# A two-level Strassen matmul: the product S3 x T3 by seven quarter products too, four weight quarters fetched again from DRAM, half of C scaled at the end

## The chip, the core and the metric

The kernel runs on one core of a Trainium2 chip. The metric is the device time of one execution, in microseconds. Before the change it is 1456.46 us, the median of three runs (1455.99 to 1456.82).

## The reference

```python
def setup_inputs():
    B, S, D = 8, 2048, 2048
    return {
        "x": np.random.randn(B, S, D).astype(np.float32),
        "w": np.random.randn(D, D).astype(np.float32),
    }

def reference(x, w):
    cs = np.cumsum(x, axis=1)
    diff = cs - np.concatenate([np.zeros(...), cs[:, :-1, :]], axis=1)
    return np.matmul(diff, w).astype(np.float32)
```

A running sum and the difference of neighbours cancel, so what is computed is x w: 16384 x 2048 by 2048 x 2048, in float32.

## The kernel before

**Tiles.** x is cut into 128 row tiles of 128 rows. The weights stay in SBUF as float16 sums (`W`). Four row tiles make a group, named g, h, k, l. g and h are the upper half of the outer Strassen scheme's A, k and l the lower one; the columns of x give the other division. After 12 tiles that are worked by other functions, 29 groups (class `Group`) remain.

**A group.** The outer scheme has seven products, P1 to P7. Each is 256 x 1024 by 1024 x 1024 and is worked either whole (`Group.whole`, 32 matmuls of 128x512) or by an inner Strassen scheme: seven quarter products p1 to p7 of four matmuls each (`quarter`, L570), with four small sums s1 to s4 of quarter rows (`small_sums`, L1001). P1 to P5 are worked by seven, P6 (S2 x T2) and P7 (S3 x T3) whole.

**Weight quarters.** An inner scheme needs sums of weight quarters. Most stand in `W` or `inner`. Six of them are made anew for each group by one VectorE operation of 128x2048 into the buffer `flow` (`fill_by`, L934; steps `P1.fp4`, `P2.fp4`, `P3.fp2`, `P4.fp4`, `P5.fp4`, `P5.fp5`) and read by the quarter product of that name.

**Results.** A 128x512 piece of C starts as a scaled copy out of a PSUM bank (`keep`, ScalarE, L580), takes further products by scaled adds (`add`, VectorE, L583: c = bank * u + c), and is stored by `put` (L594). `merge` (L1027) adds a copy of one bank to another bank, and `copy` (L1020) takes such a copy, where one product serves several sums (`by_seven`, P1 and P5).

**Rows of x.** `load` fetches a tile in two halves of 512 KB, the first to one of three places of the buffer `F`, the second to one of two others (L101). `weigh` takes the sum of magnitudes (ScalarE), `scale_of` a maximum and its reciprocal (VectorE), `unit_of` the factor for C (GpSimd), `narrow` writes float16 in place (ScalarE), `turn` transposes by DMA.

**What sets the order.** `ORDER` (L1195) is a list of step names, written out, that is gone through once per group; `+1` or `+2` says how many groups ahead a step belongs. `after` chains each engine's instructions in just this order, so each engine has a fixed queue. All loads, stores and transposes are issued by SyncE (SP), in one queue too. PSUM banks are taken from and given back to `open_banks`, pieces of C to `free`, small sums to `scratch`. The last group ends by `END_ORDER`.

## Time and profile before

| | |
|---|---|
| median of three runs | 1456.46 us |
| span of the profiled execution | 1455.0 us |
| instructions | 20120 |
| HBM read, written | 150.99 MB, 134.22 MB |
| bytes moved by DMA, mean rate | 351.59 MB, 242 GB/s |

The profile is one execution. Busy time of an engine is the union of its instructions' times; times of matmuls are pipelined and their ends modelled. An instruction's line (L584) can be that of a helper: all scaled adds into C have L584, all quarter products L573, the whole products L554, the small and large sums of x L544, the fills L937, the merges in PSUM L1030. "DMA share" is the mean busy share of the core's 16 DMA engines. Each idle time names what ended it.

### The profile page before, as it was taken

The page shows a single profiled execution, that of the slowest core. Times are in us where ns is not written, and L with a number is a line of the kernel's source. Part 1 is how long each engine was busy: PE and PEld are TensorE (multiplying, and loading weights), DVE is VectorE, ACT ScalarE, POOL GpSimd, SP SyncE. Part 2 cuts the span into 40 slices and gives each one's busy share as a digit, 9 for nine tenths or more (in the row PEclk, how much of TensorE's full clock was granted, in tenths as well). Part 3 has the DMA queues.
Part 4 walks back from the last instruction along what each step waited for, and adds up shares of the span by engine and source line. Part 5 has one row for each costly group of instructions (what it writes and reads, how often), then busy time and mean ns, then how long its engine had stood idle before and what let it go on. Part 6 is the DMA issues. An engine that isn't in the chain of part 4 may idle for free.

```text
span 1455.0 us, 20120 instructions
## 1 busy us (share of the span) xinstructions
PE 1441.1 (99%) x6673; PEld 652.6 (45%) x6679; DVE 1333.3 (92%) x2302; ACT 967.5 (66%) x1446; POOL 48.6 (3%) x136
## 2 busy tenths in 40 slices
PE   8999999999999999999999999999999999999998
PEld 3444444444444444444444444444444444444443
DVE  7998899999999999999999999999999999999998
ACT  5887656676666666667666667766666766666662
POOL 0111000000000000000000000000000000000000
PEclk9999999999999999999999999999999999999999
DMA  9999868898888998878998888998878898888983
GB/s 360 367 240 299 236 171 234 248 246 232 234 237 237 248 253 230 235 236 233 260 241 233 231 228 240 260 238 241 225 235 247 247 233 239 226 244 246 253 203 123
DMA packets 377752, 351.59 MB, mean 242 GB/s; under 512 B 274800, under 2 KB 274800, under 8 KB 377520
## 3 DMA queue, kind: packets, MB, share of 16 engines
q1 hardware_dynamic: 377088, 348.47, 84.9%
q0 software_dynamic: 560, 1.84, 0.3%
q8 instruction: 52, 0.85, 0.2%
q14 instruction: 52, 0.43, 0.1%
HBM read 150.99 MB, written 134.22 MB: 196 GB/s over the span
## 4 chain that ended last, share of the span: by engine, by line
PE 96%; DMA 2%; DVE 1%; issue 0%; ACT 0%; SPq 0%; DVEq 0%; ACTq 0%
PE b L573 61%; PE b L554 32%; PE b L275 2%; DMA W<-in_w_dram 1%; DMA W<-in_x_dram 1%; DVE c L584 1%; ACT wb L259 0%; PE b L400 0%; DVE x L544 0%; SPq L219 0%; DVE b L1030 0%; DVE flow L937 0%; DVE inner L544 0%; DVE W L541 0%; ACT c L581 0%
## 5 line engine op out<-in xcount | busy, mean ns | idle before, releaser
L584 DVE SCALAR_TENSOR_TENSOR c<-b,of,c 128x512 f32<-128x512 f32 x790 | 574.1, 747 | 74.3 <-PE b L573 64.3
L554 PE MATMUL b<-W,x 128*128 128x512 f16 x2144 | 506.6, 379 | 0.0
L581 ACT ACTIVATE c<-b,of 128x512 f32<-128x512 f32 x492 | 312.6, 680 | 230.9 <-PE b L573 113.3
L573 PE MATMUL b<-W,x 128*128 128x512 f16 x1892 | 452.4, 379 | 0.8 <-ACT b L1023 0.7
L158 ACT ACTIVATE F<-F,of 128x1024 f16<-128x1024 f32 x246 | 282.2, 1147 | 174.8 <-DVE of L141 172.6
L573 PEld LDWEIGHTS <-x 128*128 128x128 f16 x2488 | 243.4, 98 | 295.3 <-issue 2.7
L554 PEld LDWEIGHTS <-x 128*128 128x128 f16 x2144 | 209.8, 98 | 253.0 <-DVE x L544 0.2
L123 ACT ACTIVATE waste<-F 128x1024 uint8<-128x1024 f32 x246 | 259.3, 1054 | 4.6 <-DMA F<-in_x_dram 2.5
L573 PEld LDWEIGHTS <-inner 128*128 128x128 f16 x1648 | 161.2, 98 | 195.6 <-issue 1.3
L573 PE MATMUL b<-W,inner 128*128 128x512 f16 x944 | 242.2, 379 | 0.9 <-DVE b L1030 0.9
L544 DVE TENSOR_TENSOR x<-x,x 128x1024 f16<-128x1024 f16 (+1 forms) x388 | 226.6, 584 | 3.3
L573 PE MATMUL b<-flow,x 128*128 128x512 f16 x588 | 150.9, 379 | 0.0
L573 PE MATMUL b<-inner 128*128 128x512 f16 x472 | 121.1, 379 | 0.0
L937 DVE TENSOR_TENSOR flow<-W 128x2048 f16<-128x2048 f16 x87 | 105.8, 1216 | 0.0
L1030 DVE TENSOR_TENSOR b<-b,c 128x512 f32<-128x512 f32 x116 | 80.6, 695 | 13.9 <-PE b L573 13.9
L147 POOL TENSOR_SCALAR of<-of,uw 128x1 f32<-128x1 f32 x124 | 43.6, 370 | 1306.7 <-DVE of L139 704.1
L937 DVE TENSOR_TENSOR flow<-W,inner 128x2048 f16<-128x2048 f16 x58 | 70.8, 1220 | 0.0
L1023 ACT COPY c<-b 128x512 f32<-128x512 f32 x58 | 33.4, 576 | 51.3 <-PE b L573 51.3
L275 PE MATMUL b<-wb,xP 128*128 128x512 bf16 x234 | 57.0, 395 | 5.3 <-ACT wb L259 3.9
L544 DVE TENSOR_TENSOR inner<-x 128x512 f16<-128x512 f16 x117 | 49.4, 422 | 2.9 <-DMA x<-F 0.9
L1023 ACT COPY b<-b 128x512 f32<-128x512 f32 x87 | 51.2, 588 | 0.5 <-PE b L573 0.5
L544 DVE TENSOR_TENSOR inner<-x,inner 128x512 f16<-128x512 f16 x117 | 49.2, 421 | 2.0
(67 smaller groups left out, 530.0 us busy)
## 6 DMA issues: line engine op xcount, KB each, us to landing
F<-in_x_dram SPq DMA_DIRECT2D x246, 512.0 KB, 5.1
out_dram<-c SPq DMA_DIRECT2D x492, 256.0 KB, 3.0
W<-in_w_dram SPq DMA_DIRECT2D x32, 512.0 KB, 9.6
W<-in_x_dram SPq DMA_DIRECT2D x16, 256.0 KB, 7.2
x<-F SPq DMA_TRANSPOSE x246, 3.4
out_dram<-o POOLq DMA_DIRECT2D x5, 256.0 KB, 4.1
out_dram<-o SPq DMA_DIRECT2D x5, 256.0 KB, 3.5
xP<-in_x_dram SPq DMA_DIRECT2D x1, 1024.0 KB, 5.1
```

The costliest lines, as they stand in the source:

```text
L123: lambda: nc.scalar.activation(waste, where[t][i], ABS, scale=1.0 / ROW, accum_out=sums_of[t][:, i : i + 1],),
L147: after("pool", lambda: nc.gpsimd.tensor_scalar(u, m, uw, None, MUL))
L158: lambda: nc.scalar.activation(narrowed(t)[:, ds(i * NH, NH)], where[t][i], COPY, scale=s),
L275: lambda: nc.tensor.matmul(ps[r][n], xP[:, r, ko, :], wb[h, ko][:, ds(n * NB, NB)], start=(ko == 0), stop=(ko == KO - 1),),
L544: after("dve", lambda: nc.vector.tensor_tensor(dst.all, p.all, q.all, op))
L554: said = nc.tensor.matmul(to[n], a[k], b[k][:, n, :], start=(first and k == 0), stop=(k == KH - 1), skip_group_check=True,)
L573: said = nc.tensor.matmul(to, a[k], b[k], start=(first and k == 0), stop=(k == 3), skip_group_check=True)
L581: after("act", lambda: nc.scalar.activation(c, p, COPY, scale=u))
L584: after("dve", lambda: nc.vector.scalar_tensor_tensor(c, p, u, c, MUL, ADD))
L937: after("dve", lambda: nc.vector.tensor_tensor(in_twos(flow), x, y, op))
L1023: after("act", lambda: nc.scalar.copy(c, p))
L1030: after("dve", lambda: nc.vector.tensor_tensor(t, p, s, ADD))
```

## The change

P7 is worked by seven quarter products: `Inner(5, ...)` gives its weight quarters, `onto` is its plan. Unlike `by_seven`, `onto` adds into banks that already hold products: p1, p5, p6 and p7 are each copied out of a bank by ScalarE (`c1`, `c5`, `c6`, `c7`) and added to other banks by VectorE (six merges `a1` to `a7k`).

P7 has three passing weight quarters, which makes nine in a group. Four (P1.p4, P2.p4, P5.p5, P7.p4) use a second buffer, the third place of `F`. In the first group they are made by VectorE as before and stored in DRAM (`kept`); in later groups the same step is a DMA from there, issued by SP. From the twelfth x tile on, the first halves of x use two places of `F` instead of three.

For eight of the sixteen pieces of C (`LATE`), in all groups but the last, `keep` is a plain copy, `add` a plain PSUM plus SBUF add, and a new step `last` on ScalarE scales the piece in SBUF before its `put`. Maximum and reciprocal of a tile become two steps, `scale` and `recip`. `ORDER` is new as a whole. In the first group two sums that turn T3's quarters into what P7 needs stand ahead of P7.fp5.

```diff
--- before.py
+++ after.py
@@ -97,8 +97,10 @@
     queue_of_x = [PLAIN, PLAIN + 2, PLAIN + 3]
     for t in range(PLAIN + 4, END, 4):
         queue_of_x += [t, t + 2, t + 1, t + 3]
+    THREE = 11
     for i, t in enumerate(queue_of_x):
-        where[t] = [F[:, i % 3, :], F[:, 3 + i % 2, :]]
+        j = i % 3 if i < THREE else (i - THREE) % 2
+        where[t] = [F[:, j, :], F[:, 3 + i % 2, :]]
     unit = {}
     sums_of = {}
     scales = {}
@@ -129,7 +131,7 @@
                     ),
                 )
 
-    def scale_of(t):
+    def scale_of(t, apart=False):
         if t < END:
             m2 = sums_of.pop(t)
             m, s, u = (m2[:, i : i + 1] for i in (2, 3, 4))
@@ -138,12 +140,18 @@
                 "dve",
                 lambda: nc.vector.tensor_scalar(m, m2[:, :1], m2[:, 1:2], TINY, ADD, MAX),
             )
+            sizes[t] = m
+            if not apart:
+                recip_of(t)
+
+    def recip_of(t):
+        if t < END:
+            s, m = scales[t], sizes[t]
             after("dve", lambda: nc.vector.reciprocal(s, m))
-            sizes[t] = m
 
     def unit_of(t):
         if t < END:
-            u, m = unit[t], sizes.pop(t)
+            u, m = unit[t], sizes[t]
             after("pool", lambda: nc.gpsimd.tensor_scalar(u, m, uw, None, MUL))
 
     def narrowed(t):
@@ -517,7 +525,7 @@
                 p1=self.t11, p2=self.t21, p3=self.t22, p4=self.Q4,
                 p5=self.Q1, p6=self.Q2, p7=self.Q3,
             )
-            return {j: pieces_of(t) for j, t in places.items()}
+            return {j: pieces_of(t) for j, t in places.items() if t is not None}
 
     passed = [flow[:, k, :] for k in range(4)]
 
@@ -931,31 +939,60 @@
         put(C21h[0], h + 1, 0)
         turn(next_l, [1])
 
-    def fill_by(op, a, b):
-        def some():
-            x, y = (in_twos(t) for t in (a, b))
-            after("dve", lambda: nc.vector.tensor_tensor(in_twos(flow), x, y, op))
-
-        return some
-
+    kept = ctx.enter_context(tc.tile_pool(name="kept", bufs=1, space=bass.MemoryType.DRAM))
+    flows = [flow, F[:, 2, :].bitcast(f16).rearrange("p (k n) -> p k n", k=4)]
+
+    class Fill:
+        def __init__(self, op, a, b, again=False):
+            self.op, self.a, self.b = op, a, b
+            self.to = flows[again]
+            self.pieces = [self.to[:, k, :] for k in range(4)]
+            self.again = None
+            self.can = again
+
+        def __call__(self):
+            if self.again is not None:
+                after("sp", lambda: nc.sync.dma_start(self.to, self.again))
+                return
+            x, y = (in_twos(t) for t in (self.a, self.b))
+            after("dve", lambda: nc.vector.tensor_tensor(in_twos(self.to), x, y, self.op))
+            if self.can:
+                self.again = kept.tile([P, 4, NB], f16, name=f"kept{len(stored)}")
+                stored.append(self)
+                after("sp", lambda: nc.sync.dma_start(self.again, self.to))
+
+    stored = []
+
+    in_7 = Inner(5, None, quarter_of(5, 0, 1), None)
     sevens = {
-        "P1": (in_1, {"p4": fill_by(SUB, quarter_of(0, 1, 0), S1_all)}),
-        "P2": (in_2, {"p4": fill_by(SUB, quarter_of(4, 1, 0), inner[:, 8:12, :])}),
-        "P3": (in_3, {"p2": fill_by(ADD, spare_of(2, 0), inner[:, 16:20, :])}),
-        "P4": (in_4, {"p4": fill_by(SUB, quarter_of(7, 1, 0), spare_of(2, 4))}),
+        "P1": (in_1, {"p4": Fill(SUB, quarter_of(0, 1, 0), S1_all, again=True)}),
+        "P2": (in_2, {"p4": Fill(SUB, quarter_of(4, 1, 0), inner[:, 8:12, :], again=True)}),
+        "P3": (in_3, {"p2": Fill(ADD, spare_of(2, 0), inner[:, 16:20, :])}),
+        "P4": (in_4, {"p4": Fill(SUB, quarter_of(7, 1, 0), spare_of(2, 4))}),
         "P5": (
             in_5,
             {
-                "p4": fill_by(SUB, quarter_of(1, 1, 0), quarter_of(6, 1, 0)),
-                "p5": fill_by(SUB, quarter_of(1, 1, 1), quarter_of(6, 1, 0)),
+                "p4": Fill(SUB, quarter_of(1, 1, 0), quarter_of(6, 1, 0)),
+                "p5": Fill(SUB, quarter_of(1, 1, 1), quarter_of(6, 1, 0), again=True),
+            },
+        ),
+        "P7": (
+            in_7,
+            {
+                "p4": Fill(SUB, quarter_of(5, 1, 0), quarter_of(5, 0, 1), again=True),
+                "p5": Fill(SUB, quarter_of(5, 1, 1), quarter_of(5, 0, 1)),
+                "p7": Fill(SUB, quarter_of(5, 0, 1), quarter_of(5, 0, 0)),
             },
         ),
     }
     open_banks = []
     scratch = list(passing)
 
+    LATE = 'C12g0 C12g1 C12h1 C12h0 C11g1 C11h1 C21g1 C21h1'.split()
+
     class Group:
         def __init__(self, g):
+            self.late = LATE if g + 4 < END else ()
             self.tiles = dict(g=g, h=g + 2, k=g + 1, l=g + 3)
             self.at = {}
             self.do = {}
@@ -990,9 +1027,8 @@
 
             def some():
                 to, a = self.bank(b, fresh), self.sums[P][j]
-                quarter(
-                    to, self.real(a), passed if j in passes else inner.weights()[j], fresh
-                )
+                weights = passes[j].pieces if j in passes else inner.weights()[j]
+                quarter(to, self.real(a), weights, fresh)
                 if isinstance(a, str):
                     self.drop(a, scratch)
 
@@ -1046,25 +1082,64 @@
             self.quarter(P, "p3", g1, False)
             self.quarter(P, "p4", h0, False)
 
+        def onto(self, P, h0, h1, g0, g1):
+            q, e = f"{P}q", f"{P}e"
+
+            def snap(name, b, let=False):
+                def some():
+                    c, p = self.take(name, free), self.at[b]
+                    after("act", lambda: nc.scalar.copy(c, p))
+                    self.close(b, let)
+
+                return some
+
+            self.quarter(P, "p1", q, True)
+            self.step(f"{P}.c1", snap(f"{P}1", q))
+            self.merge(f"{P}.a1", g0, g0, f"{P}1", let=True)
+            self.quarter(P, "p2", g0, False)
+            self.quarter(P, "p5", e, True)
+            self.step(f"{P}.c5", snap(f"{P}5", e, True))
+            self.merge(f"{P}.a5g", g1, g1, f"{P}5")
+            self.merge(f"{P}.a5h", h1, h1, f"{P}5", let=True)
+            self.quarter(P, "p3", g1, False)
+            self.quarter(P, "p6", q, False)
+            self.step(f"{P}.c6", snap(f"{P}6", q))
+            self.merge(f"{P}.a6", g1, g1, f"{P}6", let=True)
+            self.quarter(P, "p7", q, False)
+            self.step(f"{P}.c7", snap(f"{P}7", q, True))
+            self.merge(f"{P}.a7h", h1, h1, f"{P}7")
+            self.merge(f"{P}.a7k", h0, h0, f"{P}7", let=True)
+            self.quarter(P, "p4", h0, False)
+
         def row(self, c):
             return self.tiles[c[3] if c[1] == "1" else {"g": "k", "h": "l"}[c[3]]]
 
         def keep(self, c, b, let=False):
             def some():
-                keep(self.take(c, free), self.at[b], unit[self.row(c)])
+                to, p, u = self.take(c, free), self.at[b], unit[self.row(c)]
+                if c in self.late:
+                    after("act", lambda: nc.scalar.copy(to, p))
+                else:
+                    keep(to, p, u)
                 self.close(b, let)
 
             self.step(f"keep.{c}", some)
 
         def add(self, c, b, tag, let=False):
             def some():
-                add(self.at[c], self.at[b], unit[self.row(c)])
+                to, p, u = self.at[c], self.at[b], unit[self.row(c)]
+                if c in self.late:
+                    after("dve", lambda: nc.vector.tensor_tensor(to, p, to, ADD))
+                else:
+                    add(to, p, u)
                 self.close(b, let)
 
             self.step(f"add.{c}.{tag}", some)
 
         def put(self, c):
             n = 2 * (c[2] == "2") + int(c[4])
+            if c in self.late:
+                self.step(f"last.{c}", lambda: keep(self.at[c], self.at[c], unit[self.row(c)]))
             self.step(f"put.{c}", lambda: put(self.at.pop(c), self.row(c), n))
 
         def plan(self):
@@ -1074,7 +1149,8 @@
                 self.step(f"load.{c}", lambda t=t: (load(t, 0), load(t, 1)))
                 self.step(f"weigh0.{c}", weigh, t, [0])
                 self.step(f"weigh1.{c}", weigh, t, [1])
-                self.step(f"scale.{c}", scale_of, t)
+                self.step(f"scale.{c}", scale_of, t, True)
+                self.step(f"recip.{c}", recip_of, t)
                 self.step(f"unit.{c}", unit_of, t)
                 self.step(f"narrow0.{c}", narrow, t, [0])
                 self.step(f"narrow1.{c}", narrow, t, [1])
@@ -1149,7 +1225,8 @@
             self.add("C12h1", q, "q")
             self.add("C12h0", q, "q", let=True)
 
-            self.whole("P7", T3, half["g"][0], half["h"][0], *x)
+            self.small_sums("P7", A("g", 0), A("h", 0), True)
+            self.onto("P7", *x)
             for n, c in zip(x, ("C22h0", "C22h1", "C22g0", "C22g1")):
                 self.add(c, n, "x")
 
@@ -1193,32 +1270,34 @@
                     self.step(f"{P}{c}.{j}", some, a, to, j)
 
     ORDER = """
...
+    weigh1.l+1 add.C11h1.e+1 scale.l+1 keep.C11g1+1 recip.l+1 P2.p6+1 P2.p2+1 P2.p3+1
+    narrow0.l+1 add.C11g1.q+1 S1.g+1 P2.p7+1 S2.g+1 add.C11g0.v+1 P5.p1+1 narrow1.l+1
+    add.C11g1.e+1 P6g.0+1 P6g.3+1 put.C12g1+0 add.C11h1.q+1 last.C21h1+0 P2.fp4+1
+    P3.fp2+1 P5.cg+1 last.C11h1+1 keep.C11h0+1 S4.g+1 P5.p2+1 P2.p4+1 turn0.l+1
+    turn1.l+1 S1.h+1 P5.s1+1 S2.h+1 last.C21g1+0 keep.C22g0+1 P6g.1+1 P6g.2+1 P3.p2+1
+    put.C11g0+1 P5.s2+1 last.C11g1+1 add.C11h0.q+1 load.g+2 P6h.0+1 P5.s3+1 P6h.3+1
+    P6h.1+1 P6h.2+1 S4.h+1 keep.C12g0+1 add.C12g0.z+1 P5.fp5+1 S3.g+1 weigh0.g+2 P4.s1+1
+    P7.p1+1 put.C11h1+1 P7.fp5+1 weigh1.g+2 scale.g+2 S3.h+1 P5.p5+1 unit.g+2 P7.s1+1
+    put.C11g1+1 recip.g+2 put.C21h1+0 put.C11h0+1 P7.s2+1 P7.c1+1 P7.a1+1 P7.s3+1
+    P7.s4+1 narrow0.g+2 put.C21g1+0 P7.p5+1 P5.ct+1 P7.c5+1 unit.l+1 P7.fp7+1 P5.s4+1
+    P7.p6+1 P5.p6+1 P7.p2+1 P3.s1+1 P5.m1+1 keep.C12g1+1 P7.c6+1 narrow1.g+2 P7.p7+1
+    load.h+2 weigh0.h+2 P7.c7+1 P3.s2+1 P3.s3+1 weigh1.h+2 P7.fp4+1 P5.p3+1 P5.p7+1
+    P7.a5g+1 add.C22g0.x+1 P3.p1+1 P3.s4+1 P7.a6+1 P5.m2+1 keep.C12h1+1 P4.p2+1 P7.p3+1
+    add.C12g0.q+1 P3.p6+1 P5.fp4+1 turn0.g+2 keep.C22g1+1 add.C22g1.x+1 P7.a5h+1
+    add.C12g1.q+1 scale.h+2 P7.a7h+1 last.C12g0+1 put.C22g0+1 turn1.g+2 P5.p4+1
+    recip.h+2 keep.C12h0+1 keep.C22h0+1 put.C22g1+1 P7.a7k+1 P3.p3+1 P3.p7+1
+    add.C12g1.z+1 add.C12h1.q+1 P4.s2+1 put.C12g0+1 P3.p4+1 P7.p4+1 load.k+2
+    keep.C22h1+1 narrow0.h+2 add.C12h1.z+1 add.C12h0.q+1 P4.p1+1 turn0.h+2 add.C12h0.z+1
+    narrow1.h+2 add.C22h1.x+1 keep.C21g0+1 P1.p1+2 keep.C21h1+1 P3.p5+1 turn1.h+2
+    put.C22h1+1 add.C22h0.x+1 add.C21g0.x+1 add.C12g1.e+1 P4.s4+1 last.C12h0+1
+    put.C22h0+1 weigh0.k+2 P1.cg+2 weigh1.k+2 add.C12h1.e+1 P1.s1+2 P4.s3+1 P1.s2+2
+    put.C21g0+1 P4.p6+1 P1.s4+2 scale.k+2 P2.p1+2 put.C12h0+1 last.C12h1+1 P4.p5+1
+    keep.C21g1+1 add.C21h1.e+1 unit.k+2 P4.p3+1 P1.p5+2 P1.ct+2 recip.k+2 narrow0.k+2
+    add.C21g1.q+1 P1.p6+2 P1.fp4+2 keep.C11g0+2 narrow1.k+2 last.C12g1+1 P1.s3+2 P1.p2+2
+    P1.m1+2 P4.p7+1 P4.fp4+1 P1.p7+2 P1.p3+2 P4.p4+1 add.C21h1.q+1 P1.m2+2 P1.p4+2
+    load.l+2 keep.C21h0+1 add.C21g1.x+1 unit.h+2 keep.C11h1+2 put.C12h1+1 P2.s1+2
+    turn0.k+2 weigh0.l+2 add.C21h0.x+1 P2.s2+2 P2.cv+2 turn1.k+2 P2.p5+2 put.C21h0+1
+    P2.s3+2 P2.s4+2
     """
     ORDER = [(s[:-2], int(s[-2:])) for s in ORDER.split()]
     early = max(n for _, n in ORDER)
@@ -1237,10 +1316,14 @@
     open_banks += [banks[i] for i in (6, 7, 0, 1, 3, 5, 2, 4)]
     groups = [Group(g) for g in range(PLAIN + 8, END, 4)]
     for c in groups[0].tiles:
-        for s in ("load", "weigh0", "weigh1", "scale", "unit", "narrow0", "narrow1", "turn0", "turn1"):
+        for s in ("load", "weigh0", "weigh1", "scale", "recip", "unit", "narrow0", "narrow1", "turn0", "turn1"):
             del groups[0].do[f"{s}.{c}"]
     del groups[1].do["load.g"]
-    before = {"P1.s4": lambda: less(*(half_of(t, 0) for t in (in_1.Q2, in_1.t22, in_1.Q1))), "P5.s3": in_5.third}
+    def sums_of_T3():
+        less(in_7.t12, in_7.t12, in_7.t11)
+        less(in_7.Q2, in_7.t22, in_7.t12)
+
+    before = {"P7.fp5": sums_of_T3, "P1.s4": lambda: less(*(half_of(t, 0) for t in (in_1.Q2, in_1.t22, in_1.Q1))), "P5.s3": in_5.third}
     for b in range(-early, len(groups) - late):
         for name, ahead in ORDER:
             i = b + ahead
```

More of the change, by code (lines that the diff above doesn't have):

```diff
@@ L1203 @@
-    keep.C11g0+1 add.C21h1.q+0 scale.l+1 unit.l+1 narrow0.l+1 put.C22h0+0
-    put.C21h1+0 P2.p2+1 add.C11g0.v+1 P6g.0+1 P2.fp4+1 P2.p6+1 turn0.l+1
-    narrow1.l+1 turn1.l+1 keep.C11h1+1 P6g.1+1 P2.s3+1 add.C11g1.q+1 unit.k+1
-    S4.g+1 P2.p5+1 P6g.3+1 keep.C11h0+1 add.C11h1.e+1 P2.p7+1 keep.C21h0+0
-    add.C11h1.q+1 P6g.2+1 weigh0.g+2 load.h+2 add.C21h0.x+0 P5.p1+1 P2.p4+1
-    S3.g+1 keep.C12g1+1 P2.p3+1 keep.C12g0+1 add.C11h0.q+1 put.C11h0+1 P5.fp5+1
-    weigh1.g+2 S1.h+1 P7g.0+1 P5.s1+1 P7g.1+1 scale.g+2 P5.cg+1 P5.s2+1 P5.s4+1
@@ L1210 @@
-    put.C21h0+0 narrow0.g+2 narrow1.g+2 S2.h+1 P5.s3+1 P5.p2+1 P5.p5+1 P5.ct+1
-    add.C11g1.e+1 P5.fp4+1 P5.p6+1 P5.m1+1 put.C11g0+1 keep.C22g0+1 weigh0.h+2
-    weigh1.h+2 S4.h+1 P3.s1+1 put.C11h1+1 P6h.2+1 P6h.1+1 put.C11g1+1 P3.s2+1
-    P6h.3+1 P6h.0+1 keep.C12h1+1 P5.p7+1 P5.m2+1 keep.C22h1+1 S3.h+1 P3.s4+1
-    P3.s3+1 P7g.2+1 P7g.3+1 P5.p4+1 add.C22g0.x+1 P3.fp2+1 P5.p3+1 keep.C12h0+1
-    add.C12h1.z+1 P7h.0+1 load.k+2 P3.p2+1 scale.h+2 narrow0.h+2 P3.p1+1 P7h.2+1
-    put.C22g0+1 turn0.g+2 turn1.g+2 add.C12g0.z+1 weigh0.k+2 add.C12g0.q+1
@@ L1217 @@
-    put.C12g0+1 P4.fp4+1 keep.C22g1+1 P7h.1+1 P7h.3+1 add.C22g1.x+1 put.C22g1+1
-    P3.p3+1 add.C22h1.x+1 P4.s1+1 P4.s3+1 put.C22h1+1 keep.C22h0+1 P3.p6+1
-    P3.p4+1 add.C12g1.q+1 add.C12g1.z+1 turn0.h+2 add.C12h0.z+1 weigh1.k+2
-    narrow1.h+2 load.l+2 P3.p5+1 scale.k+2 P4.p2+1 P4.p1+1 keep.C21g0+1
-    keep.C21h1+1 P3.p7+1 narrow0.k+2 P1.p1+2 add.C12g1.e+1 add.C12h1.e+1 P4.s2+1
+    weigh1.l+1 add.C11h1.e+1 scale.l+1 keep.C11g1+1 recip.l+1 P2.p6+1 P2.p2+1 P2.p3+1
+    narrow0.l+1 add.C11g1.q+1 S1.g+1 P2.p7+1 S2.g+1 add.C11g0.v+1 P5.p1+1 narrow1.l+1
```

7 lines of the change are left out of this document (removed).

## The prediction

> **What bounds the kernel now.** I read the head of the page first, then windows by stage, groups by shape, the timeline of VectorE, and the DMA answers.
>
> ```profile
> span 1455.0 us, 20120 instructions
> PE 1441.1 (99%) x6673; PEld 652.6 (45%) x6679; DVE 1333.3 (92%) x2302; ACT 967.5 (66%) x1446; POOL 48.6 (3%) x136
> PEclk9999999999999999999999999999999999999999
> PE 96%; DMA 2%; DVE 1%; issue 0%; ACT 0%; SPq 0%; DVEq 0%; ACTq 0%
> ```
>
> TensorE is busy all the time at its full clock and carries 96% of the chain that ended last. The page's share is an average, so the long middle is read by itself:
>
> ```profile
> core 0: us, PE busy (x) PEld busy (x) DVE busy (x) ACT busy (x) POOL busy (x), PEclk, DMA share, GB/s
> 10.00:36.00 26.00, 23.83 (x130) 11.94 (x131) 20.25 (x21) 17.02 (x18) 0.00 (x0) 1.00 1.03 405
> 300.00:600.00 300.00, 300.00 (x1392) 135.98 (x1391) 277.61 (x492) 202.64 (x309) 7.51 (x28) 1.00 0.86 240
> 600.00:900.00 300.00, 300.00 (x1392) 136.02 (x1391) 278.43 (x491) 202.66 (x308) 6.94 (x26) 1.00 0.87 240
> 900.00:1200.00 300.00, 300.00 (x1392) 135.99 (x1391) 277.99 (x492) 201.34 (x308) 7.47 (x28) 1.00 0.85 238
> ```
>
> 1392 matmuls in 300 us without a gap: 0.2155 us each. A group of four row tiles takes 5 products by seven quarters (5 x 28) and 2 whole ones (2 x 32) = 204 matmuls, so **43.97 us a group**. VectorE is occupied 0.927 of that, 40.7 us, ScalarE 0.67, the DMA engines 0.86. So TensorE binds, with VectorE close behind.
>
> **What one VectorE instruction really costs.** Durations overlap their successors, so I take the distance from start to start where nothing was waited for:
>
> ```profile
> 708.66 0.20 DVE L139 TENSOR_SCALAR of<-of 128x1 f32<-128x1 f32 x1
> 708.89 0.16 DVE L141 RECIPROCAL of<-of 128x1 f32<-128x1 f32 x1
> 709.00 0.75 DVE L584 SCALAR_TENSOR_TENSOR c<-b,of,c 128x512 f32<-128x512 f32 x1
> 709.67 1.22 DVE L937 TENSOR_TENSOR flow<-W,inner 128x2048 f16<-128x2048 f16 x1
> 710.80 0.42 DVE L544 TENSOR_TENSOR inner<-x,x 128x512 f16<-128x512 f16 x1
> 711.14 0.75 DVE L584 SCALAR_TENSOR_TENSOR c<-b,of,c 128x512 f32<-128x512 f32 x1
> ...
> 723.30 0.69 DVE L1030 TENSOR_TENSOR b<-b,c 128x512 f32<-128x512 f32 x1
> 723.90 0.68 DVE L544 TENSOR_TENSOR x<-x,x 128x1024 f16<-128x1024 f16 x1
> 724.62 0.42 DVE L544 TENSOR_TENSOR inner<-x 128x512 f16<-128x512 f16 x1
> 725.08 0.42 DVE L544 TENSOR_TENSOR inner<-inner,x 128x512 f16<-128x512 f16 x1
> ...
> 726.59 0.68 DVE L544 TENSOR_TENSOR x<-x,x 128x1024 f16<-128x1024 f16 x1
> 727.18 0.42 DVE L544 TENSOR_TENSOR inner<-x,inner 128x512 f16<-128x512 f16 x1
> ```
>
> A scaled add into C: 709.00 to 709.67, 0.66 to 0.67. A filled weight quarter: 709.67 to 710.80, 1.13. A small f16 sum: 0.34 (710.80 to 711.14), but 0.46 when the next needs its result (724.62 to 725.08). A merge in PSUM: 0.60. A large f16 sum: 0.59 (726.59 to 727.18), 0.72 before a dependent one. Scale and reciprocal: 0.34 together, 0.23 of it the wait of the second for the first. A group before: 26 adds x 0.66 + 4 merges x 0.60 + 8 large sums x 0.59 + 20 small x 0.34 + 6 fills x 1.13 + 4 x 0.34 = 17.2 + 2.4 + 4.7 + 6.8 + 6.8 + 1.4 = **39.3 us**; the 40.7 of the windows hold 1.4 more, dependent pairs and the tails of instructions ahead of a wait.
>
> The Trainium skill ("VectorE: DVE Perf Modes", The DRAIN you can't avoid) says that a next operation does not start until the pipe has emptied, so a group would cost its full durations. That speaks against this change, which raises VectorE's count from 72 to 80. The rows disagree: the 0.75 us add at 709.00 is followed after 0.67. By the rule the group before would already have taken 44.9 us and the one after 48.6.
>
> **The change part by part, per group.**
>
> *P7 by seven.* 28 matmuls for 32: 4 x 0.2155 = 0.86 us less on the path; TensorE's floor becomes 200 x 0.2155 = 43.1. On VectorE come four small sums (1.36) and six merges (3.6); on ScalarE four copies out of PSUM.
>
> *Fills.* Nine passing quarters, four reloaded: five remain on VectorE, 1.13 less. The first group still makes all nine.
>
> *C scaled last.* 18 of the 26 adds become an unscaled PSUM plus SBUF add into SBUF. The trace has no such instruction. Its upper bound is the scaled add, 0.66 (same operands, one more); the nearest row below is the merge at 0.60, which has the same two sources and writes PSUM. I take 0.60, since it shares the operation: 1.1 us less; at 0.66 nothing. Below 0.60 no row points. Eight of the 16 first copies lose their scale and eight scalings in SBUF come to ScalarE:
>
> ```profile
> L581 ACT ACTIVATE c<-b,of 128x512 f32<-128x512 f32 x492 | 312.6, 680 | 230.9 <-PE b L573 113.3 <-issue 63.2 <-PE b L554 28.6
> L1023 ACT COPY c<-b 128x512 f32<-128x512 f32 x58 | 33.4, 576 | 51.3 <-PE b L573 51.3
> L158 ACT ACTIVATE F<-F,of 128x1024 f16<-128x1024 f32 x246 | 282.2, 1147 | 174.8 <-DVE of L141 172.6
> ```
>
> A scaling from SBUF is not in the trace; bounds are 0.57 (half of the 1147 ns narrowing) and 0.75, I take 0.68, the scaled copy. ScalarE gains 4 x 0.58 + 8 x 0.68 - 8 x 0.10 = 7.0 us on 29.6 (202.6 of each 300 us): 36.6 of 43.1, still covered. Were it not, put steps and banks would be late.
>
> *Reciprocal apart from its maximum.* The 0.23 pause gets filled by another step: up to 4 x 0.12 = 0.5 us.
>
> VectorE after: 8 x 0.66 + 18 x 0.60 + 10 x 0.60 + 8 x 0.59 + 24 x 0.34 + 5 x 1.13 + 4 x 0.22 = 5.3 + 10.8 + 6.0 + 4.7 + 8.2 + 5.7 + 0.9 = **41.5 us**, 42.9 if the whole 1.4 of before comes on top. The floor of TensorE is 43.1. VectorE's spare falls from 4.7 us a group to between 0.2 and 1.6.
>
> *Four reloads and a ring of two.* One row of the page on DMA issues, two on the tile F (issue times in ns: least, median, most; then first and last start), three windows of 2 us:
>
> ```profile
> F<-in_x_dram SPq DMA_DIRECT2D x246, 512.0 KB, 5.1
> L111 SPq DMA_DIRECT2D F<-in_x_dram x246: 328/432/1770, 48.7 to 1398.3; - x123
> DMA to landing us min/median/max: 3.1/4.6/10.2
> 708.00:710.00 2.00, 2.00 (x11) 0.88 (x9) 1.97 (x6) 1.21 (x2) 0.53 (x2) 1.00 1.00 400
> 728.00:730.00 2.00, 2.00 (x11) 0.92 (x10) 2.00 (x3) 0.00 (x0) 0.00 (x0) 1.00 0.27 94
> 742.00:744.00 2.00, 2.00 (x11) 0.94 (x10) 1.97 (x6) 2.00 (x4) 0.00 (x0) 1.00 1.36 265
> ```
>
> A reload has the size of one x load, 512 KB. At the 405 GB/s that the start reaches with all engines busy, that is 1.3 us of them, 5.2 a group: 0.86 x 43.97 + 5.2 = 43.0 us of 43.1, hardly room. But the share counts packets that wait in each other's way (1.36 above for 265 GB/s, 1.00 for 400), and there are stretches at 0.27, so I expect longer landings, not a floor. On SP a reload issues in 0.43 us but holds the loads, stores and transposes behind it until the product that reads the second buffer has ended. From that end to the next reading there are, in the written order, 9 TensorE steps for P2.p4 (7.8 us at 0.862 a step), 8 for P5.p5 (6.9), 15 for P7.p4 and 14 for P1.p4. With 0.43 to issue and 5.1 to land, two have 2.2 and 1.4 us to spare, the others over 6. The first half of each x tile now has two places instead of three, so load.g waits for the transposes of tile k; the second half already had two, so this only takes slack away. Bounds for both together: nothing, to 28 x (2.9 + 3.7) = 185 us if every tight reload took the 10.2 maximum.
>
> The Trainium skill ("DMA: Bandwidth & Descriptors", Latency and other measured facts) gives HBM access 0.2 us on average and 2 us at high load. Estimated from that page, 1.8 us more per reload would put P5.p5 0.4 us late and P2.p4 not at all; the trace shows only the spread of landings, not its cause.
>
> *Start and end.* In the first group VectorE does four more fills (4.5) and two T3 sums (2.3): 41.5 + 6.8 = 48.3 against 43.1, so up to 5 us once; below, 2 if it runs ahead. I take 4. The last group keeps the old scaling and its hand-written end.
>
> **The sum.** If nothing but TensorE bound, 29 x 0.86 = 25 us would go. With two engines within 4% of each other, in fixed orders that wait on each other, and longer landings, I take 0.4 us a group of new gaps (bounds 0 to 1.5: below, none as in the middle now; above, the whole VectorE spare of 1.6 used up). A group then takes 43.5. The profiled 1455.0 - 28 x 0.47 + 4 = 1445.8; the runs' median, 1456.46, lies 1.46 above the span, so **1447 us**.
>
> **The rivals.**
>
> *The reloads come too late (slower).* Place: P5.p5 and P2.p4. For it: share 0.86 becomes about 1 and SP is one queue. Against: the quiet stretches. It decides once the landing passes 6.5 us for P5.p5 and 7.3 for P2.p4; at 7.5 it costs 1.0 + 0.2 a group on top of the 43.5: 1447 + 28 x 1.2 = **1481 us**. The loss outweighs the matmuls from a landing of about 6.9 on.
>
> *VectorE becomes the bound.* The unscaled add costs 0.66 and the 1.4 us come back in full, with 0.6 of waits for TensorE: 41.5 + 1.1 + 1.4 + 0.6 = 44.6: 1456.5 + 28 x 0.63 + 4 = **1478 us**. For it:
>
> ```profile
> L584 DVE SCALAR_TENSOR_TENSOR c<-b,of,c 128x512 f32<-128x512 f32 x790 | 574.1, 747 | 74.3 <-PE b L573 64.3 <-ACT c L581 1.3
> L1030 DVE TENSOR_TENSOR b<-b,c 128x512 f32<-128x512 f32 x116 | 80.6, 695 | 13.9 <-PE b L573 13.9
> ```
>
> VectorE stands waiting for products already, 78 us in all. Against: some of this waiting is only spare time, and goes when VectorE is later.
>
> *The gaps eat exactly the gain.* VectorE at 42.9 with 1.0 of waits: 43.9 a group, **1456 to 1458 us**.
>
> *The change does all it says and TensorE stays gapless.* 1456.5 - 25 + 2 = **1434 us**; the far end of my own case.
>
> **How the numbers follow.** Forecast, with the gapless end: 0.52. Late reloads 0.22, VectorE 0.19, gain eaten 0.07. What can be told from no change is about 0.2%, 3 us: faster 0.52, same 0.07, slower 0.41. Both signs hold much, so beside the forecast's own range of 1433 to 1453 stands the wide one: 1432 to 1482 leaves half of the rivals' upper tails out, about 2 in 10.
>
> **What would show it.** Right: 200 matmuls a group at 0.2155 us, VectorE at 96% or more of the middle with under 1 us of waits for products a group, the new C add at 0.69 us duration, reloads landing under 6.5 us. Wrong: TensorE gaps ahead of P5.p5 or P2.p4 that name a DMA into F (late reloads); TensorE gaps that name VectorE's merges or sums while VectorE has none (VectorE bound); ScalarE's weighing waiting for x loads (the ring of two).

## The result, and the profile after

| | median | ratio to before, 95% interval |
|---|---|---|
| before | 1456.3 us (1456.0 to 1456.8, 4 runs) | |
| after | 1522.9 us (1520.2 to 1528.8, 4 runs) | 1.0461 (1.0437 to 1.0484) |

The change makes the kernel 67 us slower. Head of the page of the changed kernel: span, busy times, TensorE's granted clock, DMA by tenths and by queue, then the chain that ended last by engine and by line.

```profile
span 1518.7 us, 21107 instructions
PE 1449.8 (95%) x6563; PEld 633.4 (42%) x6563; DVE 1391.5 (92%) x2569; ACT 1152.9 (76%) x1786; POOL 63.4 (4%) x136
PEclk9999999999999999999999999999999999999999
DMA  9999779999999999999999999999999999999994
...
q1 hardware_dynamic: 393792, 409.30, 96.6%
...
DVE 36%; DMA 26%; PE 18%; ACT 11%; issue 8%; SPq 2%; DVEq 0%; ACTq 0%
DVE c L1132 11%; DMA F<-in_x_dram 10%; PE b L581 9%; DVE b L1066 8%; DMA out_dram<-c 8%; DVE c L592 6%; PE b L562 6%; DVE x L552 4%; ACT waste L125 4%; DMA x<-F 4%; DVE inner L552 4%; ACT c L589 3%; PE b L283 2%; DVE flow L958 2%; DMA W<-in_w_dram 2%
```

Before, TensorE made 96% of the chain and DMA 2%. Now TensorE makes 18%, and no engine takes its place: VectorE, DMA and ScalarE alternate. The DMA row is full nearly from end to end. The middle of the changed kernel by windows, with the columns of the windows before:

```profile
300.00:600.00 300.00, 289.13 (x1312) 126.32 (x1310) 278.37 (x533) 237.54 (x376) 10.02 (x26) 1.00 0.98 274
600.00:900.00 300.00, 287.57 (x1300) 125.28 (x1299) 276.03 (x526) 234.03 (x370) 10.52 (x26) 1.00 1.00 275
900.00:1200.00 300.00, 288.23 (x1303) 125.54 (x1302) 275.99 (x527) 234.85 (x372) 10.02 (x26) 1.00 0.99 271
```

3915 matmuls in 900 us: a group of 200 takes 46.0 us, against 43.97 with 204 before and a floor of 43.1. VectorE is occupied 0.923 of the time, 42.4 us a group, no larger a share than before. Groups of the changed kernel, by line (busy, mean ns, idle before):

```profile
L1132 DVE TENSOR_TENSOR c<-b,c 128x512 f32<-128x512 f32 x504 | 337.2, 684 | 21.8 <-ACT c L1121 16.3
L592 DVE SCALAR_TENSOR_TENSOR c<-b,of,c 128x512 f32<-128x512 f32 x286 | 206.4, 744 | 6.4 <-PE b L581 4.8
L1066 DVE TENSOR_TENSOR b<-b,c 128x512 f32<-128x512 f32 x290 | 197.1, 692 | 12.4 <-ACT c L1091 10.2
L589 ACT ACTIVATE c<-c,of 128x512 f32<-128x512 f32 x224 | 160.1, 715 | 16.4 <-DVE c L1132 16.4
```

The unscaled add has 684 ns, the merge 692, the scaling in SBUF 715. VectorE's timeline gives the add from start to start, 723.77 to 724.37:

```profile
723.77 0.68 DVE L1132 TENSOR_TENSOR c<-b,c 128x512 f32<-128x512 f32 x1
724.37 0.41 DVE L552 TENSOR_TENSOR x<-x,x 128x512 f16<-128x512 f16 x1
```

0.60 us, so the prices of the sum hold. What grew is in the DMA issues (KB each, median us from issue to landing) and in the waits (us in all, times, longest):

```profile
F<-in_x_dram SPq DMA_DIRECT2D x246, 512.0 KB, 6.6
out_dram<-c SPq DMA_DIRECT2D x492, 256.0 KB, 4.6
F<-kept SPq DMA_DIRECT2D x112, 512.0 KB, 6.0
...
x<-F SPq DMA_TRANSPOSE x246, 4.0
```

```profile
ACT waste L125 <- DMA F<-in_x_dram: 54.9, 55, 3.0
...
ACT c L1121 <- DMA out_dram<-c: 44.1, 34, 2.6
PEld L581 <- DVE inner L552: 42.2, 79, 3.8
ACT c L1091 <- DMA out_dram<-c: 39.1, 25, 2.5
DVE of L141 <- ACT waste L125: 33.6, 41, 1.5
ACT c L589 <- DMA out_dram<-c: 31.8, 36, 2.5
DVE x L552 <- DMA x<-F: 24.8, 33, 2.6
...
PE b L581 <- DVE inner L552: 13.5, 29, 3.3
...
PE b L581 <- DMA F<-kept: 12.3, 20, 1.7
```

Loads of x land after 6.6 us instead of 5.1, stores after 4.6 instead of 3.0, transposes after 4.0 instead of 3.4. TensorE waits for a reload only 12 us in all; its matmuls and weight loads wait longer, 13.5 and 42.2 us, for small sums of VectorE, and VectorE in turn for the weighing and for transposes. ScalarE waits 115 us for stores that hold the pieces of C and 55 us for x; before, these two were 0.9 and 2.5. The chain in order of time shows how such a wait reaches TensorE (start, duration, what):

```profile
742.45 0.53 SPq L603
743.07 0.40 SPq L113
743.47 0.05 issue
743.52 7.27 DMA F<-in_x_dram
750.87 1.16 ACT waste L125 x2
752.09 0.09 issue
752.18 0.70 DVE x L552
752.90 0.43 DVE inner L552
753.38 2.78 PE b L581 x12
756.21 0.75 DVE inner L552 x2
```

By its place in `ORDER` the load is load.g: held on SP behind a store, 7.3 us to land, weighed on ScalarE, then VectorE passes scale.g, behind which S3.h and P7's sums stand, and only then TensorE goes on. The x that is loaded belongs to a later group; TensorE doesn't need it yet, only the fixed queues do.

The 6.0 us of the reloads is a median of four different steps. Taken apart by step in the trace, the medians are 5.9 us for P1.p4, 4.4 for P2.p4, 7.3 for P5.p5 and 6.9 for P7.p4, and all 12.3 us of waiting are for P5.p5. In the stretch above, its reload (window 744.5 to 745) and the matmuls that read it:

```profile
L955 SPq DMA_DIRECT2D F<-kept x1: 327/327/327, 744.7 to 744.7; - x1
...
DMA to landing us min/median/max: 7.3/7.3/7.3
```

```profile
752.05 1.02 PE L581 MATMUL b<-F,inner 128*128 128x512 f16 x4 [0.49 <-DMA F<-kept]
```

In SP's queue this reload stands right behind the two halves of load.g.

### The profile page after: what moved, and what is told of

It reads as the page before. It is cut to its first block, busy times and chain, and to the rows that moved or that the text cites. A ratio compares the mean times of both kernels' runs of the same rounds, so it can differ in the third digit from the quotient of the medians.

```text
span 1518.7 us, 21107 instructions
## 1 busy us (share of the span) xinstructions
PE 1449.8 (95%) x6563; PEld 633.4 (42%) x6563; DVE 1391.5 (92%) x2569; ACT 1152.9 (76%) x1786; POOL 63.4 (4%) x136
## 4 chain that ended last, share of the span: by engine, by line
DVE 36%; DMA 26%; PE 18%; ACT 11%; issue 8%; SPq 2%; DVEq 0%; ACTq 0%
DVE c L1132 11%; DMA F<-in_x_dram 10%; PE b L581 9%; DVE b L1066 8%; DMA out_dram<-c 8%; DVE c L592 6%; PE b L562 6%; DVE x L552 4%; ACT waste L125 4%; DMA x<-F 4%; DVE inner L552 4%; ACT c L589 3%; PE b L283 2%; DVE flow L958 2%; DMA W<-in_w_dram 2%
## 5 line engine op out<-in xcount | busy, mean ns | idle before, releaser
L581 PE MATMUL b<-W,x 128*128 128x512 f16 x2124 | 515.4, 379 | 18.5 <-DVE c L1132 7.2
L581 PEld LDWEIGHTS <-x 128*128 128x128 f16 x2952 | 287.2, 98 | 388.6 <-issue 45.9
L1132 DVE TENSOR_TENSOR c<-b,c 128x512 f32<-128x512 f32 x504 | 337.2, 684 | 21.8 <-ACT c L1121 16.3
L581 PEld LDWEIGHTS <-inner 128*128 128x128 f16 x1996 | 190.0, 98 | 290.9 <-DVE inner L552 42.2
L581 PE MATMUL b<-W,inner 128*128 128x512 f16 x1176 | 290.9, 380 | 10.2 <-DVE c L1132 4.4
L562 PE MATMUL b<-W,x 128*128 128x512 f16 x1216 | 278.0, 379 | 2.3 <-DVE x L552 2.3
L589 ACT ACTIVATE c<-b,of 128x512 f32<-128x512 f32 x268 | 180.6, 680 | 57.4 <-DMA out_dram<-c 31.8
L1121 ACT COPY c<-b 128x512 f32<-128x512 f32 x224 | 130.9, 584 | 116.3 <-DVE b L1066 52.4
L592 DVE SCALAR_TENSOR_TENSOR c<-b,of,c 128x512 f32<-128x512 f32 x286 | 206.4, 744 | 6.4 <-PE b L581 4.8
L1066 DVE TENSOR_TENSOR b<-b,c 128x512 f32<-128x512 f32 x290 | 197.1, 692 | 12.4 <-ACT c L1091 10.2
L562 PEld LDWEIGHTS <-x 128*128 128x128 f16 x1216 | 118.6, 98 | 147.0 <-DVE x L552 6.5
L589 ACT ACTIVATE c<-c,of 128x512 f32<-128x512 f32 x224 | 160.1, 715 | 16.4 <-DVE c L1132 16.4
L1091 ACT COPY c<-b 128x512 f32<-128x512 f32 x116 | 69.3, 597 | 52.1 <-DMA out_dram<-c 39.1
L581 PE MATMUL b<-F,x 128*128 128x512 f16 x348 | 89.3, 379 | 0.1
```

Source lines behind the costliest of these rows:

```text
L562: said = nc.tensor.matmul(to[n], a[k], b[k][:, n, :], start=(first and k == 0), stop=(k == KH - 1), skip_group_check=True,)
L581: said = nc.tensor.matmul(to, a[k], b[k], start=(first and k == 0), stop=(k == 3), skip_group_check=True)
L589: after("act", lambda: nc.scalar.activation(c, p, COPY, scale=u))
L592: after("dve", lambda: nc.vector.scalar_tensor_tensor(c, p, u, c, MUL, ADD))
L1066: after("dve", lambda: nc.vector.tensor_tensor(t, p, s, ADD))
L1091: after("act", lambda: nc.scalar.copy(c, p))
```

## The experiments

Grouped by question; times are medians, and ratios are to the kernel before on the same chip. "The group" is 200 matmuls by the count in the windows from 300 to 1200 us (204 where P7 is whole).

### Fewer bytes, and the ring alone

`e1_half_stores`: `out2[..., ds(at * NB, NB // 2)] <- c[:, : NB // 2]` in `Group.put`.

> The changed kernel, but each store of a group's piece of C writes only its left 256 columns (the right half of C is left out in the 29 groups): 2.1 MB a group less for the DMA engines, as many bytes as the four reloads add; every instruction, wait and order stays. Theory A (the DMA engines are the bound: share 0.99 in the middle, a group 46.0 us): the time falls to near TensorE's floor of 43.1 us a group, 1435 to 1465 us. Theory B (VectorE and the fixed orders bind; the DMA share is full only because packets wait on each other): less than 10 us go, 1510 to 1523. Theory C (the latency of the reloads and the ring of two x places bind): a part goes, since landings get shorter, 1470 to 1500.

1477.9 us, 1.0153 (1.0129 to 1.0176); group 44.4. 45 us of the loss go, at a DMA share of 0.89. Not all, so the prediction of theory A is missed by 13 us; the time lies in the range of theory C, by which a part goes because landings get shorter.

`e2_small_reloads`: `self.to[:, 0, :256] <- self.again[:, 0, :256]`.

> The changed kernel, but each reload brings only 256 of its 2048 columns (64 KB for 512 KB; the rest of the buffer keeps what the reload before left there, so C is not the reference's): 1.8 MB a group less, and the reloads land early; the ring of two and all orders stay. Theory A: nearly the same as with half stores, 1435 to 1470 us. Theory B: 1510 to 1523. Theory C, reloads late: falls by what TensorE waits for reloads and what follows, to 1440 to 1480, while half stores would give less; theory C, ring of two alone: over 1500.

1495.9 us, 1.0275 (1.0254 to 1.0296). This lies in no theory's range. 27 us of the loss go, and TensorE's waits for reloads fall from 12.3 to 0.3 us, so more than half of the gain lies elsewhere. The 64 KB reloads still took 5.0 us to land (6.0 with 512 KB); by step, 2.7 us for P2.p4 and 6.4 for P5.p5, the one behind load.g, so the transfers ahead of them count for more than their own size.

`e3_before_ring_two` and `e4_before_ring_two_loads`, on the kernel before:

```diff
+    THREE = 11
...
-        where[t] = [F[:, i % 3, :], F[:, 3 + i % 2, :]]
+        j = i % 3 if i < THREE else (i - THREE) % 2
+        where[t] = [F[:, j, :], F[:, 3 + i % 2, :]]
...
-    ... turn1.h+1 add.C12h1.q+0 ... load.k+2 P3.p2+1 ... turn1.g+2 add.C12g0.z+1 ... narrow1.h+2 load.l+2 ...
+    ... turn1.h+1 load.l+1 add.C12h1.q+0 ... P3.p2+1 ... turn1.g+2 load.k+2 add.C12g0.z+1 ... narrow1.h+2 ...
...
+                if i > 0 and name in ("P1.fp4", "P2.fp4", "P5.fp5", "P7g.2"):
+                    after("sp", lambda: nc.sync.dma_start(F[:, 2, :], w[ds(0, P), ds(0, NH)]))
```

(the last two lines in e4 alone)

> The kernel before, with two places instead of three for the first halves of x from the twelfth tile on, as in the change; load.k and load.l move behind the transposes that free their place (load.l into the next group). No reload, P7 whole, C scaled as before. Theories A and B: no change or little, 1455 to 1460 us. Theory C, ring of two: slower by over 1%, over 1470.

> The kernel of the ring of two, and from the second group on four loads of 512 KB a group into the third place of F, which nobody reads, issued on SP where the fills P1.fp4, P2.fp4, P5.fp5 and the step P7g.2 stand. VectorE's work and TensorE's are those of before (spare 4.7 us a group on VectorE). Theory A: 10.5 + 2.1 MB a group need about 46 us of the DMA engines here too, so 1490 to 1520 us, though nobody waits for the loads. Theory B: 1455 to 1465. Theory C, ring of two: as the kernel without the loads.

1827.2 us, 1.2538 (1.2517 to 1.2559), and 1896.5 us, 1.3024 (1.3005 to 1.3044). The first is slower by over 1%, as theory C said of the ring, but by 25%; of the second every theory missed. The old order has no place for loads that wait for transposes: in e3 weighing waited 310 us for x, and the four loads that nobody reads add 69 us to the time. This tells what a fixed order does with a later load, and nothing of the ring in the new order, which was drawn for it; so the ring was taken away there.

### Reloads, ring, VectorE and queue one by one

`e5_no_reloads_ring_three` (`e6_no_reloads_ring_two` without the last two changes, of `flows` and `THREE`):

```diff
         def __call__(self):
+            if self.can:
+                self.pieces = pieces_of(quarter_of(5, 0, 0))
+                return
...
-    flows = [flow, F[:, 2, :].bitcast(f16).rearrange("p (k n) -> p k n", k=4)]
+    flows = [flow, flow]
-    THREE = 11
+    THREE = END
```

> The changed kernel with no reload and no second buffer: the four products P1.p4, P2.p4, P5.p5, P7.p4 read a standing quarter of W instead (C is not the reference's), and the first halves of x have three places as before. Engine instructions of a group, their order and their other waits stay; DMA bytes are those of before. Half stores (1478 us) and small reloads (1496) left 35 to 55 us above 1435 to 1445, so bytes are not all. Theory A (only DMA throughput): as small reloads, 1470 to 1500. Theory C (x comes too late through two places, on top of the throughput): 1435 to 1455. Theory B (VectorE and the fixed orders for the rest): 1470 to 1500.

> As the kernel without reloads, but with the two places for the first halves of x as in the change. Theory C (ring of two): 1480 to 1496, like small reloads, and 25 us or more above the ring of three. Theory that the reloads' place in SP's queue is the rest: 1435 to 1460, and no more than 5 us from the ring of three. Theory B: both kernels at 1470 to 1500, within 5 us.

1485.7 us, 1.0201 (1.0186 to 1.0216), and 1488.6 us, 1.0224 (1.0209 to 1.0240). Both lie between 1470 and 1500 and within 5 us of each other, as theory B said. Without reloads the ring is worth 3 us at most. The reloads are worth 34 (1522.9 - 1488.6), and 27 of these come back with small ones already. Some 50 us above the 1434 of a gapless TensorE remain without any extra byte (e5 takes 44.9 us a group). Landings stay long too; the issues of e5:

```profile
F<-in_x_dram SPq DMA_DIRECT2D x246, 512.0 KB, 6.1
out_dram<-c SPq DMA_DIRECT2D x492, 256.0 KB, 4.2
...
x<-F SPq DMA_TRANSPOSE x246, 3.5
```

At the old bytes and a share of 0.88, loads of x take 6.1 us (5.1 before, 6.6 with the change) and stores 4.2 (3.0 and 4.6). So the larger part of their longer landings comes with the rest of the change, not with the reloads.

`e7_all_scaled_adds` on the changed kernel and `e11_no_reloads_scaled` on e5: `LATE = ()`.

> The changed kernel with C scaled as before (LATE empty): VectorE +18 x 0.06 = 1.1 us a group, ScalarE -5 us (no last scalings, scaled keeps again). Theory B (VectorE on the path in the changed kernel): slower, 1540 to 1555. Theory A (DMA throughput) and C: within 5 us of 1523, or some us faster, as pieces of C are stored without the last step and come free sooner.

> The kernel without reloads and with three x places, with all adds of C scaled (LATE empty): VectorE +18 x 0.06 = 1.1 us a group. With reloads this made no difference (1519 and 1523 us). Theory B' (VectorE's chain binds once the DMA engines have room): +15 to +35 us, 1500 to 1520. Rival (pieces of C and landings): 1470 to 1488, since the pieces come free without the last step.

1519.4 us, 1.0428 (1.0408 to 1.0447): no loss, as theories A and C said, though VectorE has some 30 us more work. Without reloads 1492.3 us, 1.0246 (1.0231 to 1.0261): 7 us more, half of the least that theory B' expected and a little above its rival's range. Scaling C last brought nothing to the kernel as changed.

`e8_reloads_pool_queue`: `after("pool", lambda: nc.gpsimd.dma_start(self.to, self.again))`.

> The changed kernel with the reloads issued by GpSimd instead of SP, so that loads, stores and transposes are no longer held behind a reload that waits for TensorE (SP waits 50 us for products and 27 us for landings ahead of reloads). Theory that the place in SP's queue costs: 10 to 40 us faster, 1480 to 1513. Theory A: within 5 us of 1523.

1572.7 us, 1.0804 (1.0767 to 1.0842). GpSimd's queue waited 502 us for products and TensorE 59 us for reloads. Both expectations missed. The other transfers, with SP to themselves, landed somewhat sooner (x 6.2 us, stores 4.2, transposes 3.7), which did not make up for that. Since GpSimd's queue also makes the factors of C, the run says that this is the worse place, and leaves open what SP's order costs.

`e9_no_fills_no_reloads`: e5 with all nine quarters read from W; `e10_reloads_no_fills`: the changed kernel with five (`if not self.can:` ahead of the VectorE fill).

> The kernel without reloads and with three x places (1486 us), and now also without the five fills that VectorE makes per group: all nine passing quarters are read from a standing quarter of W (C is not the reference's). VectorE 5.7 us a group less, its dependent sums, merges and adds and their order stay. Theory B' (VectorE's chain sets the 44.7 us a group once the DMA engines have room): 1438 to 1455, TensorE without gaps. Rival (pieces of C and x landings set them): 1475 to 1488.

> The changed kernel with its four reloads, but without the five fills of VectorE (those five quarters are read from a standing quarter of W; C is not the reference's). Theory A (in the changed kernel the DMA engines at a share of 0.99 set the 46 us a group): 1505 to 1523, though VectorE has 5.7 us a group less. Theory B' for the changed kernel too: 1440 to 1490.

1472.1 us, 1.0106 (1.0091 to 1.0121), and 1505.0 us, 1.0334 (1.0319 to 1.0349). Windows of e9 and of e10 (300 us each: TensorE, its weight loads, VectorE, ScalarE, GpSimd busy, clock, DMA share, GB/s):

```profile
600.00:900.00 300.00, 295.14 (x1352) 131.44 (x1351) 252.74 (x514) 244.85 (x388) 9.98 (x26) 1.00 0.89 235
```

```profile
600.00:900.00 300.00, 289.72 (x1314) 127.39 (x1312) 246.25 (x500) 233.63 (x371) 10.48 (x26) 1.00 1.01 276
```

29 x 5.7 = 164 us of VectorE's work out brought 14 us without reloads and 18 with them. VectorE, at 0.84, doesn't bind; that theory fell, though its rival's range (1475 to 1488) is missed too, by 3 us. e10 lies at the edge of theory A's range. Reloads and ring of two together cost 33 us with the fills out (e10 - e9) and 37 with them in (1522.9 - e5). The two costs nearly add up.

`e12_before_extra_stores`: the kernel before with four stores of 512 KB a group, `stored[...] <- inner[:, 4:8, :]`, at the steps of e4.

> The kernel before with four extra stores of 512 KB a group to DRAM, of a standing weight sum in inner, issued on SP at P1.fp4, P2.fp4, P5.fp5 and P7g.2 from the second group on; nobody reads them and the three x places stay. Theory A (the DMA engines cannot carry 12.6 MB a group in 44 us with these transposes): 1480 to 1520 us. Rival (they can; only the tight fixed order of the change makes landings matter): 1456 to 1462.

1470.1 us, 1.0091 (1.0074 to 1.0108), between both expectations. One of its windows:

```profile
900.00:1200.00 300.00, 298.39 (x1382) 135.04 (x1381) 275.31 (x487) 201.32 (x306) 6.95 (x26) 1.00 1.02 285
```

As many bytes as in the changed kernel (the extra ones as stores, where the change loads), and DMA engines as full, but a loss of 13 us; TensorE stays at 82% of the chain. Loads of x land after 5.9 us and stores after 4.2, about as in e5, which loses 29. The DMA engines carry 12.6 MB in 44.7 us, the group by all three windows, when the order leaves room for late landings. So a full share is not itself the bound of 46 us.

### Where the rest sits

`e13_load_g_early` (the changed kernel) and `e14_load_g_early_light` (e9):

```diff
-    ... P2.p4+1 turn0.l+1 turn1.l+1 ... put.C11g0+1 ... add.C11h0.q+1 load.g+2 P6h.0+1
+    ... P2.p4+1 load.g+2 turn0.l+1 turn1.l+1 ... put.C11g0+1 ... add.C11h0.q+1 P6h.0+1
```

> The changed kernel with one step moved: load.g stands in SP's queue ahead of the two transposes of tile l and the store put.C11g0, not behind them (about 3 us earlier). Theory D: what is left beside the DMA traffic is one loop: x load of tile g - its weighing on ScalarE - scale.g on VectorE, behind which S3.h and the sums of P7 and then TensorE wait; 1490 to 1510 us. Rival (DMA traffic alone sets the changed kernel): 1515 to 1530.

> The kernel without reloads and fills (1472 us) with load.g moved in the same way. Theory D: VectorE no longer waits 2 us a group for scale.g; 1438 to 1455 us. Rival (the wait moves on to the next late landing, the pieces of C or the second transposes): 1462 to 1475.

1597.9 us, 1.0963 (1.0939 to 1.0986), and 1470.7 us, 1.0100 (1.0076 to 1.0123). Both expectations of the first missed; of the second the rival came true. The waits of e14 name where it went:

```profile
ACT c L1094 <- PE b L581: 80.9, 31, 4.7
DVE x L552 <- DMA x<-F: 78.3, 28, 4.3
```

In e9 VectorE waited 40 us for transposes and 69 us for weighing; now it is 78 and 14. ScalarE's waits for the products of P7 that it copies (L1094) went from 13 to 81. Once a group the stall moved from scale.g to transposes; by `ORDER` the sum that waits is S1.h, which needs those of tile l, now behind load.g. In e13 that wait is 121 us. One loop alone is not the cause.

`e15_nine_pieces_load_early` (e14) and `e16_nine_pieces_light` (e9): two more pieces of C from the idle `flow`, `free += [flow[:, ds(2 * i, 2), :]... for i in range(2)]`. `e17_half_stores_light`: e9 with the edit of e1.

> The kernel without reloads and fills and with load.g early (1471 us), and nine pieces of C instead of seven (the idle flow buffer gives two). Its chain went from a store's landing (5.9 us) to ScalarE, which waits there for a free piece ahead of weighing tile l, to tile l's transposes, to S1.h and TensorE. Theory E (the seven pieces start this loop): 1436 to 1455. Rival (the loop closes another way): 1465 to 1473.

> The kernel without reloads and fills (1472 us, load.g where the change has it), with nine pieces of C. Theory E: 1440 to 1460. Rival (the x load of tile g alone holds this one): 1465 to 1473.

> The kernel without reloads and fills (1472 us), each store of a group writing only the left half of its piece (the right half of C is left out in the groups): 2.1 MB a group less, landings shorter, seven pieces of C. If landing times, of pieces and of x, are what closes the loops: 1436 to 1452, TensorE's floor of 43.1 us a group. If the order of VectorE and ScalarE alone closes them: 1462 to 1473.

1470.3 us, 1.0089 (1.0072 to 1.0106): no gain, as its rival said. 1462.4 us, 1.0040 (1.0025 to 1.0055): 10 us. 1460.2 us, 1.0022 (1.0013 to 1.0032): 12 us. The last two lie 2 to 3 us outside all their ranges. Waiting for pieces is one part; with load.g moved, another wait takes its place.

`e18_small_x_light`: e17 with `x2[..., ds(i * NH, P)]` into `where[t][i][:, :P]` from tile 20 on.

> The kernel without reloads and fills and with half stores (1460 us), and from tile 20 on each x load brings 128 of its 1024 columns (the rest of the place keeps old bits; C is not the reference's): x lands early and the DMA engines are far from full; every order stays. Theory D (late landings of x, weighed and scaled in ScalarE's and VectorE's fixed queues, are what is left): 1436 to 1448 us, TensorE's floor. Rival (the orders alone keep a group above 43.1 us): 1452 to 1461.

1443.0 us, 0.9906 (0.9889 to 0.9922). Theory D came true. Its DMA issues and one window:

```profile
out_dram<-c SPq DMA_DIRECT2D x464, 128.0 KB, 2.0
...
F<-in_x_dram SPq DMA_DIRECT2D x216, 64.0 KB, 2.1
...
x<-F SPq DMA_TRANSPOSE x246, 3.1
```

```profile
600.00:900.00 300.00, 299.01 (x1379) 134.61 (x1378) 258.12 (x525) 249.13 (x396) 8.21 (x28) 1.00 0.48 109
```

With every engine instruction of e9 in the same order, a group takes 43.5 us when x lands in 2.1 us and stores in 2.0. The instructions themselves are no faster (weighing 1.06 us in both, the unscaled add 0.68), so what went is waiting. This settles it for the kernel without fills: landing times close the loops, not the engines. It does not say how far landings alone would bring the kernel with its fills; that was not tried. No version that computes all of x w was faster than the kernel before.

The steps down from the changed kernel: reloads out 34 us, three x places 3, fills out 14, half stores 12, small x loads 17; 1523 to 1443.

## Why the prediction was wrong

*What held.* TensorE bound before, and 200 matmuls need 43.1 us: the lightest kernel reaches 43.5. The unscaled add costs 0.60, as taken. ScalarE, 36.6 us predicted, is busy 235.5 of 300 us, 36.1 a group. VectorE was not the bound: it is busy 42.4 us a group, within the 41.5 to 42.9 of the sum, where the rival needed 44.6. (Its instructions go from 72 to 81 a group by the sum's own terms, not to 80.)

*What failed.* The step "longer landings, not a floor", with **0.4 us a group of new gaps** and a bound of 1.5; they are 46.0 - 43.1 = 2.9. I priced late landings only at the two tight reloads, where TensorE itself reads what lands. There they cost 12 us in all. The term that was missing is every other transfer: loads of x, stores that free pieces of C, and transposes. They stand in loops of SP's, ScalarE's and VectorE's fixed queues that come round once a group, and I judged "this only takes slack away" without adding up one loop. Nor did I ask what the rest of the change, a new `ORDER` above all, does to landings at the old traffic: x goes from 5.1 to 6.1 us without any reload (e5).

Of the sum's loss of 76 us against the forecast, 34 come with the reloads (e6), 27 of them with their size (e2). The other 42 stand at the old traffic. Taken out one after the other, the third x place gives 3 us, VectorE's five fills 14, and shorter landings of stores and x 29 (e17, e18), which ends 4 us below the forecast. The landings were shortened only with reloads and fills left out, so how the 42 divide in the full kernel stays open.

*The tight reloads.* The slack of 1.4 us for P5.p5 was worked out with the median landing of one x load, 5.1. Its reload stands right behind the two halves of load.g in SP's queue and takes 7.3, past the 6.5 at which that rival was to begin. P2.p4's takes 4.4, and TensorE never waited for it.

*The size of a reload.* I took 5.2 us of all DMA engines for four, from 405 GB/s at the start. Against the same kernel without reloads (e6) they measure 0.99 x 46.0 - 0.873 x 45.0 = 6.3 us. The rate of plain loads does not hold on average beside transposes and stores: full engines moved 273 GB/s here.

*The rivals.* "Reloads come too late" had the right sign, and its condition came true for P5.p5; but its place holds 12 us of the loss, and its 1481 lay too low. "VectorE becomes the bound" fell with e7, e10 and e11, though VectorE's fills are not free (14 to 18 us). The ring of two, taken as harmless, was (3 us). Of the signs, two for "right" came true all the same: the new add at 0.68 us, and reloads under 6.5 in the median. TensorE's gaps name VectorE's sums more than reloads, but VectorE itself waits, for weighing and transposes, so that sign of a VectorE bound is not met. "ScalarE's weighing waiting for x loads" came true, 45 of the 55 us for load.g, but through the landing time, not the ring: with three places (e5) it still waits 63 us.

*Start and end* cannot be seen apart; at 28 x (46.0 - 43.97) = 57 us of the 67, some 10 us are left for both, against 4 taken.

The Trainium skill ("DMA: Bandwidth & Descriptors", Issuing engines are not separate DMA queues) says that transfers run on the same 16 engines whichever engine issues them. e8 is in line with this, though it can't show it: on GpSimd's queue the reloads still took 5.8 us to land, against 6.0 on SP's.

## What to carry to other kernels

Where engines run fixed queues, add up the loops before costing a transfer at nothing: landing, then the steps queued behind the one that waits for it, round to the transfer's next issue, once per period. A transfer that nobody needs soon still sets the pace if its first consumer stands early in an engine's queue. Ask of more DMA traffic what it does to the landing of all other transfers, and price the share from the mixed stage itself, not from plain loads.
